# Separate buffers for the substitution and for 1 / rms, a fifth tmp buffer, and one more turn between making and using a level of the attention scores

## The chip, the cores and the metric

One core of a Trainium2 chip runs the whole program. The metric is device time in microseconds (us), the median of several executions. A profile of one execution shows what each engine did: TensorE (PE, with its weight loads PEld), VectorE (DVE), ScalarE (ACT), GpSimd (POOL) and the DMA queues.

## The reference

A trunk of two pre-norm residual layers over 256 positions of width 2048, in float32. Each sublayer takes h = RMSNorm(x) * (1 + scale) + shift and adds gate * f(h) to x, where shift, scale and gate are linear in SiLU(c).

- Layer 0: one input projection feeds latent attention (8 heads) and a gated delta rule (8 heads of 128, chunks of 64), whose chunks need a triangular solve; both outputs go through one output projection.
- Layer 1: gated linear attention (GLA), 4 heads with keys of 256 and values of 512; the scores of a pair of positions are sums over channels of q * k * exp(b_i - b_j), with b the running sum of log gates.
- After each mixer a SwiGLU FFN of width 5632; at the end one more RMSNorm.

```python
def rms_norm(x, gain):
    xf = x.astype(jnp.float32)
    y = xf * lax.rsqrt(jnp.mean(xf * xf, axis=-1, keepdims=True) + EPS)
    return (y * gain.astype(jnp.float32)).astype(x.dtype)
...
    def step(state, inp):
        q_c, k_c, v_c, b_c = inp
        o_inter = jnp.einsum('bhcd,bhde->bhce', q_c * jnp.exp(b_c), state)
        rel = jnp.exp(jnp.where(causal, b_c[:, :, :, None, :] - b_c[:, :, None, :, :], -jnp.inf))
        scores = jnp.einsum('bhid,bhjd,bhijd->bhij', q_c, k_c, rel)
        o = o_inter + jnp.einsum('bhij,bhje->bhie', scores, v_c)
```

## The kernel before, in words

Everything lies transposed: channels on the 128 partitions, the 256 positions in the free dimension. A weight block is loaded by a DMA on SP's queue (raw, 4 x 128 rows by 512 columns), split by ACT into a rounded part hi (line 253) and by DVE into the rest lo (line 254), and multiplied in float32r passes: hi by both halves of the activations and lo by their high half. Products gather in four PSUM accumulators (acc); small matmuls use three others (sm). In the second half of the program `join` (line 278) empties an accumulator: a copy on ACT (line 280), then an addition on DVE.

**The order.** The program is written as Python generators, and each `yield` ends a step. `weave(main, back, n)` (line 83) runs n steps of a background generator for each step (a turn) of the main one. In a projection (`stream_T`, line 283) a turn is one block of 128 output columns over four blocks of 128 input channels. The written order is then handed to a planner (line 1669, `schedule_with_timeline_sim=True`), which decides by times of its own in which order each engine gets its instructions; each engine executes its own order strictly in turn. A tile takes a free buffer of its tag and gives it back behind its last reader; where none is free, the instruction that writes the tile waits, and everything behind it on that engine.

**Buffers named in the change.** `tmp` (line 162) gives scratch tiles of up to 128x512 floats, four in all. Most short-lived work takes from these four: the attention's probabilities p and their transposes pT, rotary products, the delta rule's blocks, `rstd` (line 226: w and y), the squares for RMS sums (`x_square`, line 508), `h_tile` (line 534), and the GLA scores. The column sums of a modulation (`ada_rows`, line 449) are copied into a tmp by line 457 and stay there until `ada_end` (line 460) has multiplied them, some background steps later. The tag `ss` has one buffer, 128x256, which holds the running sum of squares in `x_square` and `x_out`; `sv` has twelve small ones.

**The delta rule's substitution** (`gdn_blocks`, line 933) inverts 64 triangular 16x16 blocks at once on POOL: 15 steps, each a product w into a tmp and a subtraction that reads it. It is braided with the local products of the other half or with `gdn_merge` (line 963), whose copies at lines 1015, 1017, 1019 and 1036 run on ACT, and all of it is woven with the attention (`attend`, line 1223; transposes at line 1248, copy at line 1250) and the projections.

**The GLA scores** (`gla_scores`, line 1410) are made in eight levels for each of the four heads. `prepare(lv)` writes differences of b into a tmp e (DVE), takes Exp in place (ACT), and multiplies k by it into a second tmp and q by it in place (DVE). A level's eight matmuls (four at the last) go into an sm, and a predicated copy (line 1464) takes them into S. The next level is prepared ahead of the present one's matmuls:

```python
for n, lv in enumerate(levels):
    ke, qe = nxt
    if n + 1 < len(levels):
        nxt = prepare(levels[n + 1])
    ps = s.sm()
...
    yield
```

The values follow two heads later (`gla_pv`, line 1472): for each of four blocks two or three matmuls, a copy (line 1488), a square and a sum of squares by PE, and at the end `rstd`. `run` weaves all four heads' scores and values into the projection `gla_in` (line 1335) at R3 = 0.4 steps a turn. What is left of `gla_in` then has 33 turns (the second half of q and k), 64 (v) and 64 (the output gate), 161 in all.

Of the kernel before, what the change touches and what calls it, by code (L numbers as in the profile page):

```python
# [9 lines left out]
F32 = mybir.dt.float32  # L10
# [9 lines left out]
T = 256  # L20
# [88 lines left out]
W0, W1 = 3, 5  # L109
SG, SK = 1, 5  # L110
RS = (2.5, 2.5, 4, 0, 0)
RF0, RG, RF1, R3, NF = 1.5, 0.5, 0.5, 0.4, 0
RO = 1.5
PS = (1, 2, 3)
NB = 0.3
# [14 lines left out]
class Trunk:  # L130
# [29 lines left out]
        return s.dp.tile(list(shape), dt, tag="d", name=s.nm("d"))  # L160

    def tmp(s, shape=(128, 512), dt=F32):
        return s.tp.tile(list(shape), dt, tag="tmp", name=s.nm("tmp"))

    def sv(s, shape):
        return s.tp.tile(list(shape), F32, tag="sv", name=s.nm("sv"), bufs=12)
# [58 lines left out]

    def rstd(s, out, ss, n, eps=EPS):

        w = s.tmp(out.shape)
        y = s.tmp(out.shape)
        s.act(y, ss, AF.Ln, scale=1.0 / n, bias=s.eps[:out.shape[0]])  # L230
        s.ts(w, ss, -0.5 / n, ALU.mult, -0.5 * eps, ALU.add)
        s.act(y, y, AF.Exp, scale=-0.5)
        s.tt(w, w, y, ALU.mult)
        s.tt(w, w, y, ALU.mult)
        s.stt(out, w, 1.5, y, ALU.add, ALU.mult)
# [697 lines left out]
    def gdn_blocks(s, half):  # L933


        nc = s.nc
        lt = s.d((64, 16, 16))
        nc.gpsimd.dma_start(lt, s.lt[half].rearrange("u (b r) -> (u b) r", b=8)[:, :2048].rearrange(
            "l (j i) -> l j i", i=128)[:, :, :16])
        tr = s.d((64, 2, 16, 16))  # L940
        t = tr[:, 0]
        nc.gpsimd.memset(t, 0.0)
        nc.gpsimd.memset(t.rearrange("l i c -> l (i c)")[:, 0:256:17], 1.0)
        for _ in range(W0):
            yield
        for k in range(15):
            n, m = 15 - k, k + 1
            w = s.tmp((64, 16, 16))[:, :n, :m]
            s.tt(w, lt[:, k, m:].unsqueeze(2).broadcast_to([64, n, m]),
                 t[:, k, :m].unsqueeze(1).broadcast_to([64, n, m]), ALU.mult, nc.gpsimd if SG else None)  # L950
            s.tt(t[:, m:, :m], t[:, m:, :m], w, ALU.subtract, nc.gpsimd if SG else None)
            if k % SK == SK - 1:
                yield
        nc.scalar.copy(tr[:, 1], t.rearrange("l i c -> l c i"))
        blk = s.drp.tile([2, 64 * 256], F32, name=s.nm("blk"))
        nc.gpsimd.dma_start(blk.rearrange("a (l r) -> l a r", l=64), tr.rearrange("l a i c -> l a (i c)"))
        s.tc16[half] = s.d((128, 2, 8, 16))
        for a in range(2):
            nc.gpsimd.dma_start(s.tc16[half][:, a], blk[a].rearrange("(u b j i) -> (b j) u i", u=8, b=8, i=16))
        for _ in range(W1):  # L960
            yield
# [448 lines left out]
    def gla_scores(s, hh):  # L1410

        nc = s.nc
        pb = s.sm()
        for dt in range(2):
            c0 = (hh % 2) * 256 + dt * 128
            for t in range(2):
                s.mm(pb[:, dt * 256 + t * 128:][:, :128], s.ls[hh // 2, t][:, c0:c0 + 128], s.c("u"))
        b = s.d()
        nc.scalar.copy(b, pb)
        q, k = s.gq[hh], s.gk[hh]  # L1420
        S = s.d((128, 3, 128))
        Sd = S[:, 0:3:2, :]
        ps = s.sm()
        for t in range(2):
            for dt in range(2):
                tk = slice(t * 128, (t + 1) * 128)
                s.mm(ps[:, tk], k[:, dt, tk], q[:, dt, tk], dt == 0, dt == 1)
        s.tt(Sd, ps[:, :T].rearrange("p (t i) -> p t i", t=2), s.c("ident").unsqueeze(1).broadcast_to([128, 2, 128]),
             ALU.mult)
        yield  # L1430
        def prepare(lv):

            e = s.tmp()
            nb = 512 // (2 * lv)
            bv = b.rearrange("p (n e i) -> p n e i", e=2, i=lv)
            ev = e.rearrange("p (n e i) -> p n e i", e=2, i=lv)
            bm = bv[:, :, 0, lv - 1:lv].broadcast_to([128, nb, lv])
            s.tt(ev[:, :, 0], bm, bv[:, :, 0], ALU.subtract)
            if lv < 128:
                s.tt(ev[:, :, 1], bv[:, :, 1], bm, ALU.subtract)  # L1440
            else:
                nc.vector.tensor_copy(ev[:, :, 1], bv[:, :, 1])
            s.act(e, e, AF.Exp)
            ke = s.tmp((128, 2, T))
            e2 = e.rearrange("p (d t) -> p d t", d=2)
            s.tt(ke, k, e2, ALU.mult)
            s.tt(e2, q, e2, ALU.mult)
            return ke, e2

        levels = (1, 2, 4, 8, 16, 32, 64, 128)  # L1450
        nxt = prepare(1)
        yield
        for n, lv in enumerate(levels):
            ke, qe = nxt
            if n + 1 < len(levels):
                nxt = prepare(levels[n + 1])
            ps = s.sm()
            if lv < 128:
                for t in range(2):
                    for dt in range(2):  # L1460
                        tk = slice(t * 128, (t + 1) * 128)
                        s.mm(ps[:, tk], ke[:, dt, tk], qe[:, dt, tk], dt == 0, dt == 1)
                m = s.c(f"m{lv}").bitcast(U32).unsqueeze(1).broadcast_to([128, 2, 128])
                nc.vector.copy_predicated(Sd, m, ps[:, :T].rearrange("p (t i) -> p t i", t=2))
            else:
                for dt in range(2):
                    s.mm(ps[:, 0:128], ke[:, dt, 0:128], qe[:, dt, 128:256], dt == 0, dt == 1)
                nc.scalar.copy(S[:, 1], ps[:, 0:128])
            yield
        s.S[hh] = S  # L1470
# [203 lines left out]
```

## Time and profile before

| what | value |
|---|---|
| median of 3 runs | 2623.21 us (2622.59 to 2624.29) |
| the profiled execution: its time, its span | 2622.07 us, 2620.3 us |
| PE busy, PEld busy | 2552.7 us (97%), 2285.0 us (87%) |
| DVE, ACT, POOL busy | 1768.3 us (67%), 1193.8 us (46%), 97.6 us (4%) |
| granted PE clock, mean | 0.983 |
| DMA | 622.31 MB, mean 237 GB/s |

The span runs from the first to the last instruction; the execution's own time is 1.8 us more. Busy shares are means over stages with different limits. A granted clock of 1 is 2.4 GHz, the lower level is 1.2 GHz. In a timeline row the first number is the start, the second the duration (of a merged row: from the first start to the last end), and the brackets hold the idle time of that engine just before it and the instruction that ended it. All matmuls carry line 190, all DVE additions, subtractions and products line 193.

### The profile page before, as it was taken

To read this page: it belongs to the slowest core of one execution; us is meant where nothing else is said; L and a number is where in the kernel's file an instruction comes from. 1 tells how busy PE (TensorE), PEld (TensorE's weight loads), DVE (VectorE), ACT (ScalarE), POOL (GpSimd) and SP (SyncE) were. 2 spreads that over 40 slices of the span, in tenths; PEclk is the share of its full clock that TensorE was granted. 3 is DMA by queue.
4 is the path that set the end of the run, shared out by engine and by line. 5 is a ranking of instruction groups with operands and counts; after the bars stand their busy time and mean duration, and the time that the engine had idled before them with its cause. 6 is when DMAs were issued, how large, how long until landed. Compare 5 with 4: busy or idle time off the path is not lost.

```text
span 2620.3 us, 43320 instructions
## 1 busy us (share of the span) xinstructions
PE 2552.7 (97%) x17914; PEld 2285.0 (87%) x17914; DVE 1768.3 (67%) x2455; ACT 1193.8 (46%) x1809; POOL 97.6 (4%) x154
## 2 busy tenths in 40 slices
PE   8999998999999999999998989999999999999998
PEld 5799876799999999999998878878788888888887
DVE  3667654688778777777778777766655655655555
ACT  3435664445433343334345534564544344444344
POOL 0000014001000000000001000001000000000001
PEclk9999998899999999999999999999999999999999
DMA  9975567675979888878885545435455555555553
GB/s 349 351 290 167 212 251 255 261 286 205 341 276 352 310 312 313 323 298 324 308 326 191 203 166 197 166 120 193 161 190 186 189 191 190 182 191 193 177 193 113
DMA packets 262259, 622.31 MB, mean 237 GB/s; under 512 B 17119, under 2 KB 28012, under 8 KB 241582
## 3 DMA queue, kind: packets, MB, share of 16 engines
q1 hardware_dynamic: 259902, 608.32, 65.5%
q0 software_dynamic: 1968, 11.14, 1.2%
q8 instruction: 141, 2.31, 0.3%
q14 instruction: 56, 0.46, 0.0%
q10 hardware_dynamic: 192, 0.08, 0.0%
HBM read 616.09 MB, written 3.41 MB: 236 GB/s over the span
## 4 chain that ended last, share of the span: by engine, by line
PE 93%; DVE 3%; ACT 1%; DMA 1%; issue 1%; POOL 0%; SPq 0%; DVEq 0%; ACTq 0%; POOLq 0%
PE acc L190 85%; PE sm L190 5%; PE pa L190 2%; DVE lo L193 1%; ACT hi L253 1%; DMA araw<-in_ada_w 0%; DVE ada L200 0%; DVE tmp L193 0%; ACT tmp L203 0%; DVE d L193 0%; DMA d<-in_x 0%; POOL ss L193 0%; DMA d<-in_ada_w 0%; DMA d<-in_norm_g 0%; DVE x L200 0%
## 5 line engine op out<-in xcount | busy, mean ns | idle before, releaser
L190 PE MATMUL acc<-d,hi 128*128 128x256 f32 (+2 forms) x9120 | 2138.9, 321 | 16.4 <-DVE d L200 9.2
L190 PE MATMUL acc<-d,lo 128*128 128x256 f32 x6000 | 1642.8, 283 | 3.2 <-DVE lo L193 3.2
L190 PEld LDWEIGHTS acc<-d,hi 128*128 128x128 f32 (+1 forms) x9120 | 1500.7, 191 | 164.7 <-issue 20.6
L193 DVE TENSOR_TENSOR lo<-raw,hi 128x1024 fp32r<-128x1024 f32 (+2 forms) x801 | 945.2, 1204 | 576.1 <-ACT hi L253 560.6
L253 ACT CAST hi<-raw 128x1024 fp32r<-128x1024 f32 x776 | 786.0, 1047 | 991.6 <-PE acc L190 845.9
L190 PEld LDWEIGHTS acc<-d,lo 128*128 128x128 f32 x6000 | 1138.5, 191 | 30.9 <-DVE lo L193 5.4
L200 DVE SCALAR_TENSOR_TENSOR ada<-araw,sc,ada 128x1024 f32<-128x1024 f32 x240 | 299.8, 1287 | 6.3 <-DMA araw<-in_ada_w 6.2
L200 DVE SCALAR_TENSOR_TENSOR x<-acc,mod,x 128x256 f32<-128x256 f32 x272 | 119.8, 478 | 42.5 <-PE acc L190 41.6
L193 DVE TENSOR_TENSOR d<-acc,d 128x256 f32<-128x256 f32 (+1 forms) x200 | 93.2, 474 | 74.1 <-PE acc L190 52.0
L190 PE MATMUL acc<-hi,d 128*128 128x512 f32 (+1 forms) x320 | 96.0, 379 | 1.3 <-DVE d L193 1.3
L190 PE MATMUL pa<-araw,sc 128*32 128x512 f32 x480 | 75.5, 631 | 3.4 <-DMA araw<-in_ada_w 2.0
L223 ACT CAST d<-d 128x256 fp32r<-128x256 f32 x128 | 48.3, 405 | 53.2 <-DVE d L193 53.1
L193 DVE TENSOR_TENSOR d<-d,d 128x256 fp32r<-128x256 f32 (+1 forms) x155 | 61.2, 420 | 12.0 <-ACT d L223 8.2
L190 PEld LDWEIGHTS acc<-hi,d 128*128 128x128 f32 x320 | 58.5, 191 | 12.4 <-DVE d L193 1.4
L190 PE MATMUL acc<-lo,d 128*128 128x512 f32 (+1 forms) x160 | 59.8, 373 | 0.0
L203 ACT ACTIVATE d<-d 128x256 f32<-128x256 f32 (+1 forms) x94 | 45.5, 489 | 26.4 <-DVE d L200 11.6
L193 POOL TENSOR_TENSOR ss<-ss,tmp 128x256 f32<-128x256 f32 x44 | 49.1, 1115 | 72.1 <-ACT tmp L203 70.2
L193 DVE TENSOR_TENSOR tmp<-d,tmp 128x512 f32<-128x512 f32 x64 | 43.9, 687 | 10.0 <-ACT tmp L203 3.9
L514 POOL COPY ss<-tmp 128x256 f32<-128x256 f32 x3 | 2.6, 880 | 1009.5 <-ACT tmp L203 1009.5
L280 ACT COPY d<-acc 128x256 f32<-128x256 f32 x76 | 27.6, 370 | 26.5 <-PE acc L190 25.3
L203 ACT ACTIVATE d<-tmp,mod 128x256 fp32r<-128x256 f32 x64 | 29.2, 502 | 21.6 <-DVE tmp L200 16.6
L190 PEld LDWEIGHTS sm<-tmp,tmp 128*128 128x128 f32 x240 | 31.8, 193 | 8.1 <-issue 6.4
(215 smaller groups left out, 1100.1 us busy)
## 6 DMA issues: line engine op xcount, KB each, us to landing
raw<-in_ffn_w SPq DMA_DIRECT2D x264, 1024.0 KB, 5.1
araw<-in_ada_w SPq DMA_DIRECT2D x175, 1024.0 KB, 7.2
raw<-in_gla_w_in SPq DMA_DIRECT2D x48, 1024.0 KB, 5.1
raw<-in_ab_w_in SPq DMA_DIRECT2D x30, 1024.0 KB, 4.9
raw<-in_ab_w_out SPq DMA_DIRECT2D x16, 1024.0 KB, 5.3
raw<-in_gla_w_out SPq DMA_DIRECT2D x16, 1024.0 KB, 5.1
raw<-in_ab_w_in SPq DMA_DIRECT2D x20, 512.0 KB, 7.5
araw<-in_ada_w POOLq DMA_DIRECT2D x9, 1024.0 KB, 5.1
```

What stands on the lines that cost most here:

```text
L190: s.nc.tensor.matmul(out, lhsT=lhsT, rhs=rhs, start=start, stop=stop)
L193: (eng or s.nc.vector).tensor_tensor(out=out, in0=a, in1=b, op=op)
L200: return s.nc.vector.scalar_tensor_tensor(out=out, in0=a, scalar=sc, in1=b, op0=op0, op1=op1)
L203: s.nc.scalar.activation(out, a, f, **kw)
L223: s.nc.scalar.copy(hl[:, 0], x)
L253: s.nc.scalar.copy(hi[:, :n, :ncol], raw[:, a:a + n, :ncol])
L280: s.nc.scalar.copy(out, ps[:, T:])
L514: s.nc.gpsimd.tensor_copy(s.ss, q)
```

## The change

`tmp` gets five buffers. A new function `row` gives tiles of the tag `ss` (one buffer). `rstd` takes w from `row` and uses its own output as y where the result has 256 columns; it takes both from `sv` where the result has at most 8; only the delta rule's norm (512 columns) still takes two tmps. The substitution's w comes from `row`. In the GLA scores a `yield` follows `prepare` of the next level, ahead of the present level's matmuls, and R3 goes from 0.4 to 0.6.

```diff
-RF0, RG, RF1, R3, NF = 1.5, 0.5, 0.5, 0.4, 0
+RF0, RG, RF1, R3, NF = 1.5, 0.5, 0.5, 0.6, 0
...
     def tmp(s, shape=(128, 512), dt=F32):
-        return s.tp.tile(list(shape), dt, tag="tmp", name=s.nm("tmp"))
+        return s.tp.tile(list(shape), dt, tag="tmp", name=s.nm("tmp"), bufs=5)
+
+    def row(s, shape=(128, T)):
+        return s.tp.tile(list(shape), F32, tag="ss", name=s.nm("ss"), bufs=1)
...
     def rstd(s, out, ss, n, eps=EPS):
 
-        w = s.tmp(out.shape)
-        y = s.tmp(out.shape)
+        n1 = out.shape[-1]
+        w = s.sv(out.shape) if n1 <= 8 else s.row() if n1 == T else s.tmp(out.shape)
+        y = out if n1 == T else s.sv(out.shape) if n1 <= 8 else s.tmp(out.shape)
...
         for k in range(15):
             n, m = 15 - k, k + 1
-            w = s.tmp((64, 16, 16))[:, :n, :m]
+            w = s.row((64, 16, 16))[:, :n, :m]
...
             ke, qe = nxt
             if n + 1 < len(levels):
                 nxt = prepare(levels[n + 1])
+                yield
             ps = s.sm()
```

## Rows read from the trace of the kernel before

**Rows 1.** The page's head and its first part: busy us (share) and instructions.

```profile
span 2620.3 us, 43320 instructions
PE 2552.7 (97%) x17914; PEld 2285.0 (87%) x17914; DVE 1768.3 (67%) x2455; ACT 1193.8 (46%) x1809; POOL 97.6 (4%) x154
```

**Rows 2.** Table by stretch: length, busy us of each engine, granted clock, DMA.

```profile
200.00:360.00 160.00, 160.00 (x1239) 141.98 (x1238) 109.14 (x215) 97.46 (x170) 0.86 (x1) 1.00 0.58 200
360.00:460.00 100.00, 92.12 (x822) 68.23 (x821) 52.81 (x114) 51.24 (x144) 38.02 (x87) 0.93 0.69 250
```

**Rows 3.** Table by stretch, the four stretches C, D, A and B.

```profile
428.00:450.00 22.00, 14.78 (x191) 10.43 (x191) 11.44 (x20) 10.97 (x33) 11.46 (x21) 0.69 0.80 308
480.00:498.00 18.00, 15.74 (x119) 9.82 (x112) 13.24 (x27) 11.40 (x36) 0.00 (x0) 0.63 0.62 230
1516.00:1538.00 22.00, 14.69 (x70) 12.87 (x69) 14.39 (x27) 5.56 (x11) 0.53 (x1) 0.77 0.24 78
1726.00:1738.00 12.00, 7.32 (x28) 6.15 (x27) 8.04 (x18) 9.98 (x20) 0.00 (x0) 0.72 0.26 87
```

**Rows 4.** Timeline of PE, 1516 to 1532 us.

```profile
1521.40 1.16 PE L190 MATMUL sm<-tmp,tmp 128*128 128x128 f32 x8 [4.16 <-DVE tmp L193]
1524.43 1.19 PE L190 MATMUL sm<-tmp,tmp 128*128 128x128 f32 x4 [1.87 <-DVE tmp L193]
...
1531.25 0.50 PE L190 MATMUL acc<-hi,d 128*128 128x512 f32 x1 [1.29 <-DVE d L193]
```

**Rows 5.** Timeline of DVE, 1489 to 1524 us.

```profile
1513.26 0.69 DVE L193 TENSOR_TENSOR tmp<-d,tmp 128x512 f32<-128x512 f32 x1 [0.58 <-PE sm L190]
...
1522.65 0.69 DVE L193 TENSOR_TENSOR tmp<-d,tmp 128x512 f32<-128x512 f32 x1 [1.40 <-PE sm L190]
```

**Rows 6.** Instructions on tmp tiles, 1380 to 1540: durations in ns, first and last start.

```profile
L457 ACT COPY tmp<-sm x1: 588/588/588, 1390.4 to 1390.4; 128x512 f32<-128x512 f32 x1
...
L190 PE MATMUL sm<-cst,tmp x8: 214/253/354, 1528.8 to 1529.7; 128*128 128x4 f32 x8
```

**Rows 7.** PE's score matmuls of heads 0, 1 and 3, the same view by head.

```profile
L190 PE MATMUL sm<-tmp,tmp x60: 270/275/553, 1478.2 to 1525.2; 128*128 128x128 f32 x60
...
L190 PE MATMUL sm<-tmp,tmp x60: 270/275/275, 1538.2 to 1576.2; 128*128 128x128 f32 x60
...
L190 PE MATMUL sm<-tmp,tmp x60: 270/275/275, 1675.8 to 1714.8; 128*128 128x128 f32 x60
```

**Rows 8.** Timeline of ACT, 1524 to 1532 us.

```profile
1529.37 1.18 ACT L280 COPY d<-acc 128x256 f32<-128x256 f32 x4
```

**Rows 9.** Timeline of PE, 430 to 441 us.

```profile
437.80 0.47 PE L190 MATMUL sm<-tmp,d 32*32 32x32 f32 x5 [4.75 <-ACT tmp L1015]
```

**Rows 10.** Timelines of POOL and ACT, 424 to 439 us.

```profile
428.33 0.78 POOL L193 TENSOR_TENSOR tmp<-d,d 64x63 f32<-64x63 f32 x1 [3.33 <-PE acc L1248]
...
437.19 0.26 POOL L193 TENSOR_TENSOR d<-d,tmp 64x39 f32<-64x39 f32 x1
...
437.49 0.54 ACT L1015 COPY tmp<-sm 32x128 f32<-32x128 f32 x2 [3.00 <-POOL d L193]
```

**Rows 11.** Timeline of DVE, 1403.5 to 1406.2 us.

```profile
1404.76 0.88 DVE L193 TENSOR_TENSOR tmp<-tmp,tmp 128x256 f32<-128x256 f32 x2
```

**Rows 12.** Timelines of PE and ACT, 480 to 491 us.

```profile
483.71 1.12 PE L190 MATMUL sm<-tmp,cst 128*128 128x512 f32 x2 [2.26 <-ACT tmp L203]
...
490.00 0.53 ACT L1015 COPY tmp<-sm 32x128 f32<-32x128 f32 x2 [3.23 <-PE acc L1248]
```

**Rows 13.** Timelines of ACT and PE, 1724 to 1733 us.

```profile
1726.39 1.28 ACT L203 ACT_TABLE_LOAD   x1
1727.68 0.47 ACT L203 ACTIVATE tmp<-sm,eps 128x256 f32<-128x256 f32 x1
1728.17 1.28 ACT L203 ACT_TABLE_LOAD   x1
...
1731.88 1.22 PE L190 MATMUL sm<-tmp,cst 128*128 128x256 f32 x2 [4.68 <-ACT tmp L203]
```

## The prediction

> **What bounds the kernel now.** I read the engines' shares first: TensorE (PE) is busy for 2552.7 of 2620.3 us [rows 1], so the kernel is bound by PE, and what can be won is PE's idle time (67.6 us) and the time in which its clock stands at the lower of its two levels (1.2 instead of 2.4 GHz). The table by stretch shows where they are [rows 2]: between 200 and 360 us PE never stops, from 360 on (end of the attention and of the delta rule) it does, and there the granted clock is below 1. Then I looked for PE's gaps one by one in the timeline and took the four worst stretches together, two at the end of the first layer's mixer and two in the second's [rows 3]. In each the cost is idle time plus busy time x (1 - granted clock), since a stretch at half rate with mean clock c loses about 1 - c of its work:
>
> - C, 428 to 450: 22 - 14.78 = 7.2 idle, 14.78 x 0.31 = 4.6 by the clock, 11.8 us.
> - D, 480 to 498: 2.3 idle, 15.74 x 0.37 = 5.8, 8.1 us.
> - A, 1516 to 1538: 7.3 idle, 14.69 x 0.23 = 3.4, 10.7 us.
> - B, 1726 to 1738: 4.7 idle, 7.32 x 0.28 = 2.0, 6.7 us.
>
> Together 37.3 us, 1.4% of the time. The rest of PE's idle time lies at the start, at the end and where a norm separates two projections, in chains whose instructions stay as they are.
>
> **Gap A is a shortage of tmp buffers.** PE's timeline shows the matmuls of level 64 at 1521.40 and of level 128 at 1524.43, and both wait for products of VectorE (DVE), 4.16 and 1.87 us [rows 4]. DVE's products k x exp, in turn, wait on PE's score matmuls, right behind those of the level before: at 1513.26 and 1522.65 [rows 5], the second 0.09 us after level 64's end. By the code no product of level n + 1 needs the matmuls of level n; what it needs is a buffer that they free. Two levels are alive at once, two buffers each, so four would do. But the column sums that line 457 copied at 1390.4 sit in a tmp until the matmuls that read them at 1528.8 [rows 6]: during the whole of head 0 only three of the four are left. The head's first and last level start 47.0 us apart; in heads 1 and 3, which have all four, it is 38.0 and 39.0 [rows 7]. So head 0 falls behind, the 33 turns of q and k end, and PE has only the scores' chain left. Behind it the four copies of line 280 wait on ScalarE (ACT), at 1529.37 after the scores' own copies [rows 8], and the v projection starts at 1531.25.
>
> **Gap C is the substitution's buffers.** PE runs at 437.80 after 4.75 us of idle, released by the copy of line 1015 [rows 9]. That copy, 437.49, waited 3.00 us for GpSimd (POOL), whose substitution step ended at 437.19 + 0.26 [rows 10]: the copy wanted a tmp that held a step's product w. The other way round, w waited 3.33 us at 428.33 for PE's transposes of the attention [rows 10].
>
> **The change part by part.**
>
> *Instructions.* None is added, removed or resized but for where w and y lie: 0 us. On memory it is one 128x512 buffer more.
>
> *rstd in row.* One row buffer makes the q and kv norms of the first layer follow one another (second w after the first result). That is four DVE operations on 128x256; two of them take 0.88 us in the norm at 1404 [rows 11], four 1.8, between 200 and 360 us, where PE is busy 160.00 of 160.00 [rows 2]; without that cover it would cost those 1.8 us. At the start of an FFN the chain Ln, multiply, Exp, multiply, multiply is the same with y = out: 0. x_square's sum and w share the row, but the sum is read before w is made, and the next sum starts after the layer's last rstd: 0.
>
> *Substitution in row.* All 15 steps write and read w on POOL itself, which is in order, so one buffer costs nothing. The copy of line 1015 loses its 3.00 us wait. Behind it on ACT stand the attention's copies (line 1250), and PE waits for it. Bounds: 0 (another tmp is late instead) to 11.8 (all of C). I take 3.00 idle and the same share of the clock, 3.0 / 7.2 x 4.6 = 1.9: **-4.9 us**. Next late there: line 1017's copies, which stand before it on ACT.
>
> *Five tmps.* Head 0 gets four for its levels again. Bounds for A: 0 to 10.7. I take the two waits on DVE, 4.16 + 1.87 = 6.0, and 6.0 / 7.3 of the clock's 3.4, 2.8: **-8.8 us**. The last 1.29 (accumulators not yet emptied) I leave in. In D line 1015's copy waits 3.23 us for the transposes too [rows 12], but PE was working then; its own 2.26 waits for a square that stands in ACT's queue behind line 1017's copies. Bounds -8.1 to +2.3 (the gap once more); nearest to a data chain, so 0.
>
> *The extra turn and the pace.* Before, a head is 10 steps (5 more for its values), 60 in all, at 0.4 a turn 150 of the 161 turns; after, 17 + 5, 88 in all, at 0.6 147 turns. So the heads end at the same place, but a level takes 2 / 0.6 = 3.3 turns instead of 2.5, and from making to use pass three steps, 5 turns, instead of 2.5. Heads 1 to 3 show no gap with four buffers, so nothing is to be had there: 0. The values run at 1.7 turns a step instead of 2.5, which meets gap B: PE waits 4.68 for a square, ACT having spent 1726.39 to 1729.45 on Ln and two table loads of 1.28 for the norm of head 2 [rows 13]. Bounds -6.7 (B goes, the values being further ahead) to +6.7 (one more such gap, at head 1's values); I take 0, the ACT work being the same.
>
> In the rows no drain stands beside a load: the Ln starts 0.01 us after the first load's end, and the second load 0.02 us after the Ln's [rows 13]. The Trainium skill (ScalarE: Activation LUTs, What ACT_TABLE_LOAD costs) has 2.66 us for a switch, load and drain; by it one more pair of switches in front of PE would be 5.3 us, by the row 2.6.
>
> **The sum.** -4.9 - 8.8 = -13.7. The profiled execution took 2622.07 us (span 2620.3 and 1.8 around it), so 2608.4; the median of the three runs is 1.1 above it, so **2609.5 us**. About 0.2% (5.2 us) can be told from no change.
>
> **The rivals.**
>
> *More goes (2597).* One buffer early in a chain moves all behind it: A whole (10.7), C whole (11.8), half of D (4.0): -26.5, 2596.7. For it: the three stretches each show a wait on a tmp [rows 5, 10, 12]. Against: planned orders change as a whole, and D's own chain is data.
>
> *Only the substitution (2618).* A's cause is that the stream has ended, and whoever is last waits. Head 0 now ends after 17 / 0.6 = 28 turns instead of 25 of the 33 before the v projection, so its margin shrinks from 8 to 5 turns. Then A stays and C's -4.9 is all: 2623.2 - 4.9 = 2618.3. Against it: 47 against 38 us [rows 7]. The Trainium skill (Perfetto Trace Analysis, Optimization Strategy) reads a gap as missing buffers when the same one repeats along a stretch. A stands once in four heads, so by that rule a cause other than tmp would be likelier; the trace answers with the one long-held buffer [rows 6].
>
> *Slower (2632).* The extra turn makes each level's pair live through 5 turns, so the heads drift further behind the projections rather than less. Today head 3's last level starts at 1714.8 [rows 7], 12.4 us before PE's gap at 1731.88 - 4.68 = 1727.2 [rows 13]. If each head slips by one level, 38.0 / 7 = 5.4 us, head 3 is 21.6 us later; it decides from 12.4 us of slip on. Then 9.2 us stand uncovered at B, with B's share of clock (2.0 / 4.7) 13.2; A stays, C gives 4.9: +8.3, 2631.5. For it: head 0's margin above. Against: five buffers loosen the chain that makes the slip.
>
> *Nothing (2623).* The orders come out of a planner that decides by its own times; a new tie may cost elsewhere what A and C give.
>
> **How the numbers follow.** Forecast 0.50, more 0.17, only the substitution 0.15, slower 0.10, nothing 0.08. Faster: the first two, and half of the third, which lies on the border: 0.75. Same: its other half and the last: 0.15. Slower 0.10. The range goes from 2595, a little beyond "more", to 2625, past "nothing"; the slower case and a rest at the bottom are left out.
>
> **What would show it.** A right: the first to last matmuls of head 0 stand about 38 us apart, the waits 4.16 and 1.87 are gone and the clock from 1510 to 1540 is near 1. C right: POOL's w never waits, line 1015's copy follows line 1017's at once, and PE's 4.75 shrinks to under 2. Wrong: PE idle before scores in heads 1 to 3, a gap at B longer than 4.7, or more idle PE in 360 to 580.

## The result and the profile after

| | before | after |
|---|---|---|
| median of 4 runs, us | 2623.47 (2622.59 to 2624.29) | 2592.61 (2589.08 to 2595.77) |
| the profiled execution, its span, us | 2622.07, 2620.3 | 2595.77, 2593.6 |

The ratio is 0.9882, 95% interval [0.9865, 0.9899]: 30.9 us faster. The forecast was 13.7 us faster, and the measured time lies 2.4 us below the lower end of its range, 2595. The profiled execution of the changed kernel was the slowest of its four, so the spans of the two profiles differ by 26.7 us, and that is what can be traced.

The first page of the changed kernel answers to [rows 1]:

```profile
span 2593.6 us, 43272 instructions
PE 2539.1 (98%) x17914; PEld 2279.7 (88%) x17914; DVE 1768.3 (68%) x2455; ACT 1188.6 (46%) x1806; POOL 98.9 (4%) x154
```

PE's idle time fell from 67.6 to 54.5 us, its busy time by 13.6: the same number of matmuls at a mean granted clock of 0.988 instead of 0.983. I cut the profiles at three places that every kernel has: PE's sums of squares ahead of the first FFN, the first projection of GLA and the first of the second FFN. The stages in us, each from one profiled execution:

```
kernel        what it has of the change         first mixer  first FFN   GLA    rest    span
before        nothing                              613.4       794.5    452.4   760.0   2620.3
after         all                                  604.4       795.5    432.3   761.3   2593.6
e1_buffers    all buffers, no turn, R3 0.4         604.4       795.7    431.1   760.8   2592.1
e2_turn       turn and R3 0.6 alone                614.8       793.8    444.3   760.8   2613.7
e3_tmp5       five tmps alone                      618.6       794.7    432.5   760.9   2606.7
e4_row        1 / rms and substitution             610.5       793.9    445.4   760.8   2610.5
e5_ev_own     before, line 457's sums own buffer   609.5       794.1    441.4   760.0   2605.0
e10_rstd      1 / rms alone                        609.6       793.6    446.2   761.2   2610.6
e11_sub       substitution alone                   598.4       794.5    455.5   761.2   2609.6
e9_pace04     all, but R3 0.4                      604.9       794.7    454.2   760.4   2614.2
e7_no_turn    all but the turn                     602.4       794.9    438.1   760.3   2595.6
e12_local     one own buffer at each gap           600.5       793.5    434.1   761.4   2589.4
e13_sub_tmp5  substitution and five tmps           605.1       795.0    431.0   759.9   2591.0
```

The time comes from the two mixers (9.0 and 20.1 us); the other two parts took 1.0 and 1.3 longer. How far a stage can be trusted, the table shows itself: `before`, `e2_turn` and `e5_ev_own` have the same first mixer in the source, and it takes 613.4, 614.8 and 609.5 us. And executions of one kernel differ: the kernel before, run beside experiments 5 to 8, took 2616.09 to 2625.45 us. A difference of some 5 us in one stage of one profile is therefore not shown by itself; a gap that comes or goes in the timeline is.

The table by stretch of the changed kernel, PE alone (length, PE's busy time and matmuls, granted clock, DMA share, GB/s):

```profile
420.00:440.00 20.00, 16.80 (x273) 0.83 0.80 297
440.00:460.00 20.00, 19.78 (x224) 1.00 0.65 230
460.00:480.00 20.00, 17.70 (x210) 0.83 0.65 253
480.00:500.00 20.00, 17.86 (x163) 0.91 0.83 315
1500.00:1520.00 20.00, 20.00 (x123) 1.00 0.53 171
1680.00:1700.00 20.00, 20.00 (x121) 1.00 0.49 159
1700.00:1720.00 20.00, 20.00 (x116) 1.00 0.32 107
```

**A is gone.** The timeline of PE, head 0's first level, its last two, and between them the matmuls that read line 457's column sums (line 461 now):

```profile
1469.49 1.05 PE L193 MATMUL sm<-tmp,tmp 128*128 128x128 f32 x8
...
1502.73 1.05 PE L193 MATMUL sm<-tmp,tmp 128*128 128x128 f32 x8
1505.02 0.95 PE L193 MATMUL sm<-cst,tmp 128*128 128x4 f32 x8
1507.30 0.61 PE L193 MATMUL sm<-tmp,tmp 128*128 128x128 f32 x4
```

From the first matmul of the first level to the start of the last are 37.8 us, 46.3 in the kernel before (1478.16 to 1524.43), though the sums are still held almost to the end; the waits of 4.16 and 1.87 us [rows 4] are gone, and the clock is 1.00.

**B is gone, and ACT's table loads are not.** ScalarE's timeline around the norm of head 2 answers to [rows 13]:

```profile
1694.49 1.28 ACT L206 ACT_TABLE_LOAD   x1
1698.46 0.47 ACT L206 ACTIVATE d<-sm,eps 128x256 f32<-128x256 f32 x1 [2.68 <-PE sm L193]
1698.95 1.28 ACT L206 ACT_TABLE_LOAD   x1
1700.25 0.42 ACT L206 ACTIVATE d<-d 128x256 f32<-128x256 f32 x1
1700.57 0.36 ACT L1493 COPY d<-sm 128x256 f32<-128x256 f32 x1
1700.96 0.42 ACT L206 ACTIVATE tmp<-d 128x256 f32<-128x256 f32 x1
```

The two loads of 1.28 us stand there as before; the norm now writes into d, the next square starts 0.71 us after the norm's Exp has started (1.89 before), and PE is busy 20.00 of 20.00 on both sides (above).

**C is smaller.** PE's timeline (first row), ScalarE's (the next three) and GpSimd's (the last two) at the end of the first mixer:

```profile
431.85 0.47 PE L193 MATMUL sm<-tmp,d 32*32 32x32 f32 x5 [3.19 <-ACT tmp L1019]
```
```profile
429.60 1.22 ACT L1021 COPY d<-d 32x128 f32<-32x128 f32 x4
430.89 0.62 ACT L958 COPY d<-d 64x256 f32<-64x256 f32 x1
431.54 0.54 ACT L1019 COPY tmp<-sm 32x128 f32<-32x128 f32 x2
```
```profile
428.57 1.08 POOL L196 TENSOR_TENSOR ss<-d,d 64x15 f32<-64x15 f32 x1
429.74 1.12 POOL L196 TENSOR_TENSOR d<-d,ss 64x15 f32<-64x15 f32 x1
```

GpSimd's steps follow each other without a wait, and the copy that had waited 3.00 us [rows 10] (line 1019 now) follows ACT's other copies at once. But those, and the substitution's own result copy (line 958), now stand in front of it, so PE's 4.75 us [rows 9] fell to 3.19 only. The other copies end at 430.82, and line 958's copy reads what the last substitution step has written, which ends at 430.86; the copy starts at 430.89. So PE waits for both here, by the order of ScalarE's copies and no longer by a buffer. With the measure of the forecast (idle plus busy x (1 - clock), in 20 us stretches) the loss between 400 and 460 us fell from 13.5 to 6.3 us.

**D stayed.** The same measure gives 8.3 us between 460 and 500 before and 9.1 after; its two gaps are now

```profile
472.74 2.08 PE L193 MATMUL sm<-tmp,cst 128*128 128x512 f32 x2 [2.30 <-ACT tmp L206]
487.54 1.06 PE L193 MATMUL pa<-araw,sc 128*32 128x512 f32 x8 [2.14 <-DMA araw<-in_ada_w]
```

How the loss divides between C and D is one order's affair: kernel 1 below, with the same first mixer in the source, loses 11.2 us between 400 and 460 and 3.6 between 460 and 500. The sum is what the two have in common: 21.8 us before, 15.3 in the changed kernel, 14.8 in kernel 1.

### The profile page after: what moved, and what is told of

It is laid out like the page before. It is cut to its first block, busy times and chain, and to the rows that moved or that the text cites. A ratio compares the mean times of both kernels' runs of the same rounds, so it can differ in the third digit from the quotient of the medians.

```text
span 2593.6 us, 43272 instructions
## 1 busy us (share of the span) xinstructions
PE 2539.1 (98%) x17914; PEld 2279.7 (88%) x17914; DVE 1768.3 (68%) x2455; ACT 1188.6 (46%) x1806; POOL 98.9 (4%) x154
## 4 chain that ended last, share of the span: by engine, by line
PE 93%; DVE 2%; DMA 1%; issue 1%; ACT 1%; POOL 1%; SPq 0%; DVEq 0%; POOLq 0%; ACTq 0%
PE acc L193 85%; PE sm L193 5%; PE pa L193 2%; DVE lo L196 1%; DMA araw<-in_ada_w 1%; ACT hi L257 0%; POOL ss L196 0%; DVE ada L203 0%; POOL d L196 0%; DMA d<-in_norm_g 0%; DMA d<-in_ada_w 0%; DVE tmp L203 0%; DVE tmp L196 0%; DMA d<-in_x 0%; DVE x L203 0%
## 5 line engine op out<-in xcount | busy, mean ns | idle before, releaser
L193 PEld LDWEIGHTS sm<-d,d 32*32 32x32 f32 (+2 forms) x368 | 30.1, 146 | 9.1 <-issue 5.7
```

Of the source, the lines that this page charges most:

```text
L193: s.nc.tensor.matmul(out, lhsT=lhsT, rhs=rhs, start=start, stop=stop)
```

## The experiments

Theory P: the buffers make the gain. Its rivals: turn and pace make it; one buffer edit makes it all. Times are medians. Ratios are to the kernel before, run beside each (its medians were 2619.27 to 2620.53 us), with 95% intervals; they are worked out from all executions and can differ a little from the quotient of the medians.

**1. All buffers, no turn, old pace** (the changed kernel without this):

```diff
-RF0, RG, RF1, R3, NF = 1.5, 0.5, 0.5, 0.6, 0
+RF0, RG, RF1, R3, NF = 1.5, 0.5, 0.5, 0.4, 0
...
-                yield
```

> Both buffer edits, without the extra yield and with R3 = 0.4. Theory P (the prediction: the buffers make the gain, gap A is the held tmp, C the substitution's w): head 0's levels within 38 us, no gap A, C as in the changed kernel, B stays: about 2623 - 10.7 - 9 = 2603. Theory T (the turn makes the gain in the second layer, the buffers only C): A and B both stay, C goes: 2623 - 9 = 2614. Theory both (A needs the fifth buffer, B the turn): as P.

2593.52 us, ratio 0.9895 [0.9880, 0.9909]; all stages within 1.2 us of the changed kernel's. The buffers are the gain. The time is 9.5 us below theory P's 2603, which let B stay: B went too.

**2. Turn and pace alone**, over the old buffers (the two edits above put into the kernel before).

> The extra yield and R3 = 0.6 alone, with the old buffers (four tmps, w and y among them). Theory P: head 0 has three tmps, so A stays or grows and C stays: 2620 to 2627. Theory T: the second layer's mixer is 20 us shorter as in the changed kernel and C stays: about 2603.

2611.55 us, 0.9964 [0.9951, 0.9977]; GLA 8.1 us shorter. The time lies between the two theories' values. PE has no gap over 0.3 us left between 1490 and 1535. Head 0 takes even longer from its first level to its last (50.4 us), but none of its levels waits for its products any more: with three steps between making and using a level, three tmps do. That reading of the cause is argued from the order and was not tried by itself. One new gap, 2.74 us at 1635.54, stands in front of head 2's last two levels. B stays, by PE's timeline:

```profile
1724.45 1.22 PE L190 MATMUL sm<-tmp,cst 128*128 128x256 f32 x2 [4.24 <-ACT tmp L203]
```

So turn and buffers are two remedies for A, and beside the buffers the turn adds nothing (1).

**3. Five tmps alone** (`bufs=5` in `tmp`).

> Only the fifth tmp. Theory P: A goes (-10.7), C in part since the substitution's w still takes one (-3 to -9): 2604 to 2610. Theory T: the second layer keeps A and B, 2614 to 2623.

2608.0 us, 0.9949 [0.9932, 0.9966]. GLA takes 432.5 us, the changed kernel's time: one buffer heals A and B. The first mixer gets 5.2 us longer, which is no more than kernels with the same first mixer differ (5.3, above). The time lies in theory P's range (2604 to 2610) by luck: P had B stay and C go in part.

**4. 1 / rms and the substitution, with four tmps** (the edits of `rstd` and of the substitution's w).

> Only the separate buffers of rstd and of the substitution, with four tmps and R3 = 0.4. Theory P: C goes (-5 to -9), A stays as head 0 has three tmps: 2614 to 2618. Theory T says the same here; if w was not the cause of C, 2623.

2617.28 us, 0.9985 [0.9975, 0.9994]. GLA is 7.0 us shorter, B being gone and A still there. The first mixer gains 2.9 only: PE's gap at C is down to 0.24 us, but between 440 and 500 us 17.5 us are lost in other gaps (12.8 before). The time lies in theory P's range, by another path. The profiled execution, 2612.70 us, was among the shortest of ten (2612.26 to 2620.38).

**5. The held column sums alone in a buffer of their own:**

```diff
-        ev = s.tmp()
+        ev = s.tp.tile([128, 512], F32, tag="ev", name=s.nm("ev"), bufs=1)
```

> The kernel before, but the column sums of line 457 get one buffer of their own, so the scores of head 0 have four tmps again; nothing else. Theory H (gap A comes from the held column sums): head 0's levels stand 38 us apart, A goes, B and C stay: 2623 - 10.7 = about 2611. Theory N (any change of orders would have done it): A stays, within 0.2% of before.

2608.17 us, 0.9955 [0.9940, 0.9970]. GLA is 11.0 us shorter, A has no gap left, and B stands where it was:

```profile
1716.81 1.22 PE L190 MATMUL sm<-tmp,cst 128*128 128x256 f32 x2 [4.68 <-ACT tmp L203]
```

A's cause is the one long-held tmp. B is something else. The first mixer, in which this edit changes nothing, is 3.9 us shorter all the same.

**6. 1 / rms alone** (with the function `row`):

```diff
-        w = s.tmp(out.shape)
-        y = s.tmp(out.shape)
+        n1 = out.shape[-1]
+        w = s.sv(out.shape) if n1 <= 8 else s.row() if n1 == T else s.tmp(out.shape)
+        y = out if n1 == T else s.sv(out.shape) if n1 <= 8 else s.tmp(out.shape)
```

> The kernel before, but rstd takes w and y as in the changed kernel; the substitution's w stays a tmp, four tmps, R3 = 0.4. Theory R (gap B comes from rstd's two tmps, for which the next head's squares wait): B goes, A and C stay: 2623 - 6.7 = about 2616. Theory L (B comes from the table loads on ACT): B stays, 2620 to 2624.

2612.14 us, 0.9966 [0.9953, 0.9979]; GLA 6.2 us shorter. A's two waits are there, within 0.01 us, in PE's timeline:

```profile
1517.61 2.04 PE L193 MATMUL sm<-tmp,tmp 128*128 128x128 f32 x8 [4.15 <-DVE tmp L196]
...
1521.52 1.20 PE L193 MATMUL sm<-tmp,tmp 128*128 128x128 f32 x4 [1.86 <-DVE tmp L196]
```

B is gone: PE has no gap over 0.3 us between 1705 and 1740, though ScalarE still loads two tables for this norm:

```profile
1718.35 1.28 ACT L206 ACT_TABLE_LOAD   x1
1719.64 0.47 ACT L206 ACTIVATE d<-sm,eps 128x256 f32<-128x256 f32 x1
...
1720.67 1.28 ACT L206 ACT_TABLE_LOAD   x1
1721.96 0.42 ACT L206 ACTIVATE d<-d 128x256 f32<-128x256 f32 x1
1722.29 0.40 ACT L206 ACTIVATE tmp<-d 128x256 f32<-128x256 f32 x1
```

So B's cause is that the norm of head 2 holds two of four tmps (w, y) while the squares of head 3 want theirs. In the kernel before, VectorE's last step of that norm, which frees both, and the square that PE waited for are 0.10 us apart (VectorE's timeline, then ScalarE's):

```profile
1730.84 0.42 DVE L200 SCALAR_TENSOR_TENSOR d<-tmp,tmp 128x256 f32<-128x256 f32 x1
```
```profile
1730.57 0.40 ACT L1488 COPY d<-sm 128x256 f32<-128x256 f32 x1
1730.84 0.68 ACT L280 COPY d<-acc 128x256 f32<-128x256 f32 x2
1731.36 0.77 ACT L203 ACTIVATE tmp<-d 128x256 f32<-128x256 f32 x2
```

No wait shows there, because the order that the planner gave has ACT's copies in front of the square. A shortage that was planned around shows as an order. That the planner chose this order for the shortage is read from the 0.10 us; that the shortage is the cause is shown by 3, 6 and 10, which all end it.

**7. The substitution alone** (its w from `row`).

> The kernel before, but the substitution's w gets a buffer of its own; rstd as before, four tmps, R3 = 0.4. Theory P (C comes from w): the first layer is 5 to 9 us shorter, A and B stay: 2614 to 2618. Theory J (C needs the fifth tmp as well, since the attention and the merge take turns at four): 2620 to 2624.

2612.77 us, 0.9975 [0.9962, 0.9988]. The first mixer is 15.0 us shorter, more than in the changed kernel. PE's gap at C, still ended by the copy of line 1015 (1018 here), is

```profile
431.48 0.34 PE L193 MATMUL sm<-tmp,d 32*32 32x32 f32 x5 [0.64 <-ACT tmp L1018]
```

GLA keeps A and B and is 3.1 us longer.

**8. The changed kernel at the old pace** (R3 0.4).

> The changed kernel with R3 = 0.4: all buffers and the extra yield, but 88 steps at 0.4 need 220 turns where there are 161, so some 24 steps (the end of head 3's scores and the values of heads 2 and 3) are left to run without projections beside them. Theory of the tail: that costs some 25 to 40 us over the changed kernel, 2618 to 2633. If the planner fills the tail with the output projection: 2593 to 2600.

2616.02 us, 0.9982 [0.9972, 0.9992], just under the theory's 2618; GLA takes 454.2 us. With 88 steps at 0.4 a turn the heads outlast the projection. PE's timeline at its end:

```profile
1723.83 3.92 PE L193 MATMUL sm<-tmp,tmp 128*128 128x128 f32 x16 [6.46 <-DVE tmp L196]
1729.11 1.13 PE L193 MATMUL sm<-tmp,tmp 128*128 128x128 f32 x8 [1.35 <-ACT tmp L206]
1731.31 1.95 PE L193 MATMUL sm<-tmp,tmp 128*128 128x128 f32 x8 [1.08 <-ACT tmp L206]
1747.27 0.70 PE L193 MATMUL sm<-tmp,cst 128*128 128x256 f32 x2 [3.13 <-ACT tmp L206]
```

**9. The changed kernel without the turn** (R3 0.6).

> The changed kernel without the extra turn, but with its faster pace (R3 0.6). Theory (turn and pace buy nothing beside the buffers): the GLA stage within 2 us of the changed kernel's 432.3, time 2591 to 2595. Rival (at the faster pace a level needs the turn between making and use, or TensorE waits for the products): a level's matmuls follow its products at 1.7 turns, TensorE shows a gap of some tenths of a us at most of the 32 levels, the GLA stage is 5 us or more longer, time 2597 or more.

2598.9 us, 0.9919 [0.9908, 0.9931]; GLA takes 438.1 us, 5.8 more than with the turn. The rival is right in size, not in form. There is no gap at every level, but one where a head's last two levels wait for VectorE's products, and one of 1.56 us at 1665.20 for another result of VectorE:

```profile
1654.45 2.90 PE L193 MATMUL sm<-tmp,tmp 128*128 128x128 f32 x12 [3.57 <-DVE tmp L196]
```

The turn needs the pace (8), the pace needs the turn (9), and the two together are worth nothing beside the buffers (1).

**10. One own buffer at each gap**: the substitution's w as in 7, the sums as in 5, and w, y of 1 / rms out of the tmps in the GLA values only (line 1497). Four tmps, old pace.

> The kernel before with one own buffer at each of the three places and nothing else: the substitution's w in row, the column sums of line 457 in a buffer of their own, and w and y of 1 / rms out of the tmps only where the GLA values end (line 1497). Four tmps, old pace, no extra turn. Theory (each gap has its own holder of a tmp): the GLA stage falls from 452 to about 432 us, gaps A and B (4.16, 1.87 and 4.68 us) are gone; the first layer's mixer falls from 613 to about 598 us as with the substitution's buffer alone; time about 2587 us, 5 us under the changed kernel. Rival 1 (it is the number of tmps that counts, whoever holds them): with four the GLA stage stays at 440 us or more, time 2596 or more. Rival 2 (the first layer's gains depend on the whole order that the planner finds, not on one buffer): the first layer takes 604 to 612 us, time 2593 to 2601.

2597.0 us (2590.32 to 2597.32), 0.9904 [0.9891, 0.9917]. PE's table by stretch:

```profile
1500.00:1600.00 100.00, 100.00 (x518) 1.00 0.60 200
1600.00:1700.00 100.00, 97.86 (x584) 1.00 0.48 158
1700.00:1800.00 100.00, 99.46 (x570) 1.00 0.52 179
```

A and B are gone with four tmps (GLA 434.1 us), so rival 1 is out: each gap has its own holder, and any remedy that takes the holder away does. For the first mixer it stays open. In the profile it takes 600.5 us, nearer to the theory's 598 than to rival 2's 604; but the profiled execution, 2591.27 us, was one of the two shortest of five, and the median lies 10 us above the theory's 2587, in rival 2's range.

**11. The substitution and five tmps.**

> The changed kernel's two buffer edits that look largest by themselves: the substitution's w in row and five tmps; 1 / rms still takes two tmps everywhere; old pace, no extra turn. Theory: the fifth tmp heals A and B (432 us for the GLA stage, as with it alone), the substitution's buffer heals C (598 us for the first mixer): about 2587 us. Rival: the fifth tmp, which alone made the first mixer 5 us longer, takes part of C's gain again whatever 1 / rms does: first mixer 604 us or more, time 2593 or more, as the changed kernel.

2594.77 us, 0.9904 [0.9891, 0.9917]. GLA takes 431.0 us as the theory says, the first mixer 605.1 as the rival says. The fifth tmp takes nearly half of the substitution's gain back, and it does so at C: between 400 and 460 us 9.1 us are lost, against 2.1 in 7, and PE's gap there is 2.51 us. In all kernels with five tmps it is 2.5 to 3.2 (1, 3, 8, 9, 11 and the changed one), in those with four and w in `row` 0.64 at most (4, 7, 10). No version was measurably faster than the changed kernel.

## Why the prediction was too small

What theory P says of the cause holds: the buffers do it, each at its own gap. What failed were terms of the sum. By the profiles the gain is 13.0 us more than forecast; of these B is 6.7, the rest of A 1.9 and the rest of C 2.3. The other 4.2 us of the 17.2 that the medians show lie between executions and can't be traced.

- **B, taken at 0: the step that failed.** The prediction laid B to ACT's Ln and table loads and took it as unmoved, "the ACT work being the same". Taken alone (6), the edit of 1 / rms removes the gap with the loads in place, and GLA falls by 6.2 us; the prediction's bound for B was 6.7. It costed that edit in the first mixer and in the FFN, and did not ask who else takes tmps while the third user, the GLA values, runs its norm. "More goes" came nearest (2597), but left B out too, and D's half that it counted did not go.
- **A, -8.8: right in cause, short in size.** The row of the held sums [rows 6] named the cause, and experiment 5 shows it. But 1.29 us and the rest of the clock's loss were left in as something else's; they went too. All of A was 10.7 us, and 5 gives 11.0. (The prediction's 47.0 us of head 0 run to the last matmul; from level to level they are 46.3, against 37.8 after.) A wait that follows in the same stretch was late for the same reason.
- **C, -4.9: short.** The loss between 400 and 460 us fell by 7.2 (in kernel 1, with the same first mixer, by 2.3 only, and D's by 4.7). "Next late" was right (the copies now at line 1021 stand before the one waited for), the sign "under 2 us" was not: 3.19 remain. With the substitution's edit alone (7) it is 0.64: what remains comes with the fifth tmp, which the prediction did not weigh at C.
- **D, 0: right** in the changed kernel (8.3 to 9.1 us, the gap of 2.26 now 2.30). But it is no data chain alone: with four tmps and w in `row` (4, 7, 10) the gap is 0.91.
- **Turn and pace, 0: right in sum, not in reason.** "Nothing is to be had there" was said of heads 1 to 3; it is on head 0 that the pair acts: alone it ends A (2). It adds nothing because the buffers had already done so. "Slower" (heads drifting past the end of the projection) did not happen at 0.6 and did happen at 0.4 (8).
- **Only the substitution** fell: A went by buffers alone (3, 5).

By the profiles, A and B at 10.7 + 6.7 = 17.4 of GLA's 20.1 us are accounted for, and a gap of 0.94 us at 1669.92 that also went makes 18.3. In the first mixer C's 7.2, less D's 0.8, leave 2.6 of 9.0 untraced.

Two rules were weighed. The Trainium skill (Perfetto Trace Analysis, Optimization Strategy) reads a gap that repeats as a possible sign of too few buffers. Here gaps that stood once, A and B, were shortages all the same, one by a tile held for 138 us: the trace agrees on the repair, and it does not bear out what the prediction drew from the rule, that for a gap that stands once another cause is likelier. The Trainium skill (ScalarE: Activation LUTs, What ACT_TABLE_LOAD costs) has 2.66 us for a switch. The rows differ, and they decide: a load takes 1.28 us, the Exp starts 0.02 us behind it, and after the change a pair of loads costs PE no idle time.

**What stays open.** The first mixer's gains do not add. Alone, the substitution gives 15.0, 1 / rms 3.8, the fifth tmp -5.2; all three 9.0. Part of this need not be an effect of an edit at all: experiments 2 and 5 change nothing there and move it by +1.4 and -3.9, so the 3.8 of 1 / rms alone is not shown to be its own. Kernels 1, 8, 9 and the changed one, which have the same first mixer in the source, lie between 602.4 and 604.9. The 6.8 us between 7 and 11 lie at C, where the loss differs by 7.0; why ScalarE's and PE's orders there come out otherwise with a fifth tmp was not tried.

## What to carry to other kernels

For a pool of shared scratch tiles, list at each gap who holds every buffer, and for how long, the tiles held across a long stretch and the helper functions' pairs first; an engine without idle time in front of a late instruction can still be late for want of a buffer, because it was given an order that avoids the shortage. When an edit touches a helper, cost it at every caller. A and B, each with one holder, went whole, their share of the clock and the smaller neighbours with them; C, where something else stood next in line, did not. So for a gap with one cause the whole is the likelier value than the one wait that is named, if nothing else is late behind it.

## What had not been expected

**Steps of GpSimd that take as long as VectorE's.** A step of the substitution takes some 0.3 us, but those that run beside a long operation of VectorE take 1.1 to 1.3. GpSimd's timeline of the changed kernel, then VectorE's in the same 6 us:

```profile
424.94 0.28 POOL L196 TENSOR_TENSOR d<-d,ss 64x48 f32<-64x48 f32 x1
425.30 1.26 POOL L196 TENSOR_TENSOR ss<-d,d 64x39 f32<-64x39 f32 x1
426.64 0.27 POOL L196 TENSOR_TENSOR d<-d,ss 64x39 f32<-64x39 f32 x1
426.98 0.23 POOL L196 TENSOR_TENSOR ss<-d,d 64x28 f32<-64x28 f32 x1
427.29 1.21 POOL L196 TENSOR_TENSOR d<-d,ss 64x28 f32<-64x28 f32 x1
```
```profile
425.23 1.23 DVE L196 TENSOR_TENSOR lo<-raw,hi 128x1024 fp32r<-128x1024 f32 x1 [1.12 <-ACT hi L257]
427.17 1.23 DVE L196 TENSOR_TENSOR lo<-raw,hi 128x1024 fp32r<-128x1024 f32 x1 [0.71 <-ACT hi L257]
```

The two long steps shown begin 0.07 and 0.12 us behind the start of one of VectorE's and end 0.1 us behind its end: they are held until that one is done. The Trainium skill has this (SBUF — State Buffer, SBUF: two separate sides): an operation of VectorE with two SBUF inputs and one of GpSimd that reads SBUF lock the same ports, and whoever comes first has them for the whole instruction. The rows agree for the case that VectorE comes first. Six steps of this half were so held, ending 0.07 to 0.18 us behind one of VectorE's, by some 0.9 us each, 5.5 of the 16.0 us that it took (414.84 to 430.86). The last two of the six are the steps shown at C, ahead of line 958's copy.
